# Attention's queries and keys turned on VectorE during the retention stage, and the opening stage reordered

## The chip, the cores and the metric

The kernel runs on one core of one Trainium2 chip. The metric is device time in microseconds: the median of a few runs of the whole program. The profile is of one further execution.

## The reference

One layer of a streaming encoder on 1024 tokens of width 1024, with 16 meta tokens in front. All mixers read the same normalised input through one projection, and their outputs go through one output projection. Cut to what matters here:

```python
u = rms_norm(h, ln_w[l])
(cx, cb, cc, cz, cq, ckv, krope, mz, rq, rk, rv, rz) = split(u @ w_in[l])
y_conv = short_conv_mixer(cx, cb, cc, cz, ...)
# attention: 8 heads of 96, v of 64, chunk-causal mask
q = rms_norm(rms_norm(cq) @ w_uq, q_norm);  k = rms_norm(concat(k_nope, k_r), k_norm)
s = einsum('bqhd,bkhd->bhqk', rope(q), rope(k)) * 96 ** -0.5
y_mla = einsum('bhqk,bkhd->bqhd', softmax(mask(s)), v) * silu(mz)
y_ret = retention_mixer(rq, rk, rv, rz, ...)       # 4 heads of 64, a state carried from chunk to chunk
h = h + concat(y_conv, y_mla, y_ret) @ w_out[l]
```

## The kernel before

All data are float32. A product of two float32 matrices is made of three matmuls (`mm3`, L109): each operand is split into a rounded part and a rest (`split`, L100: ScalarE makes the one, VectorE or GpSimd the other by subtraction), and high x high, high x low and low x high are summed in PSUM.

The program is written as one list of steps, and the framework lays out the order of each engine's queue when the program is built: an instruction that its plan holds ready may come ahead of others that stand earlier in the text, and the text decides between ready ones. Once laid out, each queue runs strictly in its order; SP's queue issues nearly all DMAs.

The stages, in the order of the profile:

- Opening, to 55 us (L170 to L260). TensorE warms up with `NW` matmuls on zeros (L175). Then 8 blocks of the input, each with its weights, are loaded and split, and the attention gates `mz` are summed over them: blocks 0 to 3 of 128 columns by two halves g of the tokens, each with a PSUM tile of its own. Blocks (0,0), (0,1), (1,0), (1,1), (2,0) run with the loads; (2,1) and block 3 come behind (`rest`, L179). Meanwhile x is read token by token for its sums of squares; `r` is the reciprocal norm of each token, and a matmul of ones with a diagonal matrix (L243) turns four tiles of it into a row over all partitions, `rb`. L253 to L260 make the gates of `mz` and store them. The weights of the next projection, `wA`, are loaded by `load_w` (L114): four (`NA`) early, four behind the gates (L270). They share 12 buffers with the weights of `mz`.
- Projection A, 55 to 121 us (L293 to L409): latents, queries, keys and values of attention, with norm and rotation. Queries and keys are stored to DRAM token by token, as `q_s` and `k_s` (L388, L368).
- Retention, 121 to 246 us (L423 to L532). For two pairs of heads u and nine tiles of tokens t, `r_proj` makes a projection of 24 matmuls; `step()` then runs what earlier tiles left for later: `r_rope` (rotation on VectorE, then two small transposes `rtp` on TensorE, L456), `r_score`, `r_out`. The weights of u = 1 are loaded during u = 0, those of the convolution during u = 1 (L528 to L532).
- Convolution, 246 to 345 us (L535 to L602), whose last part is interleaved with the start of attention (L797 to L815).
- Attention, 345 to 530 us, 8 heads of 8 tiles (L794 to L864). For each head `load_pair` (L542) has loaded queries and keys of two heads, token by token on the partitions. `qk_t` (L662) turns 512 tokens of one head with four TensorE transposes (L668) into PSUM, and splits them from there into `qT` or `kT`; the queries are scaled by `wqk`, the product of the two norm weights, in that split. It is called four times for each head (which of q and k, which half of the tokens), for heads 2 to 7 two heads ahead, after the tiles in `QK`. `score` makes the scores of one tile, `p_t` turns the softmax, `attend` multiplies with v. Part of the output projection (`partial`) fills in.
- Output projection, to the end.

The pool `hpp` (L71) has two buffers for each of the tags "q", "k" and "v". The tag "q" is used in turn by the input blocks, the attention weights `uq`, the queries of a pair, and late outputs.

## Time and profile before

| | us |
|---|---|
| median of 3 runs | 580.33 (579.04 to 581.69) |
| the profiled execution | 581.55 |
| its span, first to last instruction | 579.8 |
| TensorE busy | 569.8 |
| VectorE busy | 330.9 |
| ScalarE busy | 255.0 |
| GpSimd busy | 224.1 |

A busy time is the time in which at least one instruction of the engine is under way. Matmuls overlap one another, so the room that one takes in TensorE's queue is the distance from its start to the next start, not its duration. In the rows PE is TensorE, DVE VectorE, ACT ScalarE, POOL GpSimd, SP the queue of DMAs; L668 is line 668 of the program; `kTp<-ident,k` says that kTp is written and ident and k are read.

### The profile page before, as it was taken

Reading aid. Unit: us, or ns where it says so; the run is one execution under the profiler, and the core shown is the slowest. Engines: PE = TensorE matmul, PEld = TensorE weight load, DVE = VectorE, ACT = ScalarE, POOL = GpSimd, SP = SyncE. Lnnn points to the kernel's source line nnn. Section 1 sums busy time; section 2 is a strip of 40 time slices with the busy share of each in tenths; the row PEclk is TensorE's granted clock in tenths of the full one; section 3 lists DMA queues with packets and bytes.
Section 4 is the critical chain, followed back from the end, with each engine's and each line's share of the span. In section 5 each row is a group of like instructions: output and inputs, shape, how many; then the busy total and the mean of one; then the engine's idle time right before and its main releaser. Section 6 shows DMA issues by size and latency. Waiting matters only on the chain.

```text
span 579.8 us, 9595 instructions
## 1 busy us (share of the span) xinstructions
PE 569.8 (98%) x3401; PEld 481.7 (83%) x3401; DVE 330.9 (57%) x761; ACT 255.0 (44%) x616; POOL 224.1 (39%) x330
## 2 busy tenths in 40 slices
PE   8999999999999999999999999999999999999997
PEld 5877899988888888898898888898888888876886
DVE  5547768888536432553332667675757857664132
ACT  6765535665234332532010438475655646543000
POOL 2023258677103220151242968443524334624000
PEclk9999999999999999999999999999999999999999
DMA  8887513274703200130030648235112223113096
GB/s 326 289 265 241 182 67 120 108 224 158 234 1 92 74 0 19 54 110 18 20 97 1 199 145 273 73 103 171 56 38 73 77 71 128 37 68 116 1 301 224
DMA packets 46657, 70.39 MB, mean 121 GB/s; under 512 B 3792, under 2 KB 21840, under 8 KB 46480
## 3 DMA queue, kind: packets, MB, share of 16 engines
q1 hardware_dynamic: 43008, 63.47, 33.8%
q10 hardware_dynamic: 3600, 6.29, 2.9%
q8 instruction: 27, 0.44, 0.3%
q14 instruction: 22, 0.18, 0.1%
HBM read 48.75 MB, written 21.00 MB: 120 GB/s over the span
## 4 chain that ended last, share of the span: by engine, by line
PE 83%; DMA 9%; DVE 3%; ACT 2%; issue 2%; POOL 0%; SPq 0%; DVEq 0%; ACTq 0%; POOLq 0%
PE r L112 16%; PE S L112 9%; PE cv L112 8%; PE part L112 7%; PE A L112 6%; PE o L765 6%; PE pTp L724 5%; PE cz L112 4%; PE cb L112 4%; DMA out<-ot 4%; PE out L112 3%; PE qps L112 3%; DMA xs<-in_xT 2%; DMA xt<-in_x 2%; PE rsp L477 1%
## 5 line engine op out<-in xcount | busy, mean ns | idle before, releaser
L702 ACT ACTIVATE pr<-S,smx 128x144 f32<-128x144 f32 (+8 forms) x72 | 50.4, 701 | 27.3 <-DVE smx L693 13.4
L693 DVE TENSOR_REDUCE smx<-S 128x1 f32<-128x144 f32 (+8 forms) x72 | 49.8, 701 | 15.7 <-PE S L112 6.3
L710 POOL TENSOR_SCALAR pm<-pr,smx 128x16 f32<-128x16 f32 x64 | 18.4, 288 | 85.2 <-DVE smx L708 61.3
L711 POOL TENSOR_SCALAR pr<-pr,smx 128x128 f32<-128x128 f32 (+3 forms) x64 | 48.1, 752 | 0.6 <-DVE smx L708 0.6
L724 PE MATMUL pTp<-ident,pr 128*128 128x128 f32 x288 | 45.4, 274 | 1.5 <-ACT pt L730 1.4
L730 ACT COPY pt<-pTp 128x512 f32<-128x512 f32 (+2 forms) x64 | 31.8, 505 | 26.3 <-PE pTp L724 24.9
L451 POOL TENSOR_SCALAR kw<-qk,con 128x64 f32<-128x64 f32 (+1 forms) x36 | 13.8, 397 | 71.7 <-DVE qk L447 58.4
L724 PEld LDWEIGHTS pTp<-ident,pr 128*128 128x128 f32 x288 | 35.0, 140 | 7.0 <-POOL wol L104 1.8
L765 PEld LDWEIGHTS o<-pt,v 128*64 128x64 f32 x448 | 26.5, 137 | 12.1 <-issue 4.7
L765 PE MATMUL o<-pt,v 128*64 128x256 f32 (+2 forms) x448 | 36.2, 309 | 0.0
L112 PE MATMUL r<-wh_r,xal 128*128 128x512 f32 (+1 forms) x80 | 30.5, 381 | 0.0
L112 PE MATMUL r<-wh_r,xah 128*128 128x512 f32 (+1 forms) x80 | 30.4, 380 | 0.0
L112 PE MATMUL part<-woh,yh 128*128 128x512 f32 x64 | 30.1, 470 | 0.0
L112 PE MATMUL r<-wl_r,xah 128*128 128x512 f32 (+1 forms) x80 | 30.0, 375 | 0.0
L882 DVE SCALAR_TENSOR_TENSOR ot<-out,xr 128x512 f32<-128x512 f32 (+1 forms) x17 | 11.2, 660 | 31.1 <-DMA out<-ot 16.8
L112 PE MATMUL r<-wl_r,xbh 128*128 128x512 f32 x64 | 26.1, 409 | 0.0
L112 PE MATMUL r<-wh_r,xbh 128*128 128x512 f32 x64 | 25.7, 401 | 0.0
L112 PE MATMUL part<-wol,yh 128*128 128x512 f32 x64 | 25.5, 399 | 0.0
L112 PE MATMUL r<-wh_r,xbl 128*128 128x512 f32 x64 | 25.5, 398 | 0.0
L112 PE MATMUL part<-woh,yl 128*128 128x512 f32 x64 | 25.2, 394 | 0.0
L773 DVE TENSOR_TENSOR ym<-o,ym 64x256 f32<-64x256 f32 x32 | 13.5, 421 | 16.7 <-PE o L767 16.2
L104 POOL TENSOR_TENSOR wol<-wos,woh 128x512 fp32r<-128x512 f32 x16 | 20.4, 1291 | 2.6 <-ACT woh L103 2.6
(295 smaller groups left out, 1716.1 us busy)
## 6 DMA issues: line engine op xcount, KB each, us to landing
xt<-in_x SPq DMA_DIRECT2D x16, 256.0 KB, 4.5
ws_r<-in_win SPq DMA_DIRECT2D x16, 256.0 KB, 3.3
ws_c<-in_win SPq DMA_DIRECT2D x16, 256.0 KB, 2.9
wos<-in_wout SPq DMA_DIRECT2D x16, 256.0 KB, 3.8
xp<-in_x SPq DMA_DIRECT2D x16, 256.0 KB, 2.7
p_s<-xp SPq DMA_DIRECT2D x16, 256.0 KB, 2.0
xr<-p_s SPq DMA_DIRECT2D x15, 256.0 KB, 4.5
out<-ot ACTq DMA_DIRECT2D x15, 256.0 KB, 4.5
```

The source lines that it names most:

```text
L104: (lo_eng or nc.vector).tensor_tensor(lo, src, hi.bitcast(F32), op=ALU.subtract)
L112: nc.tensor.matmul(out, lhsT=x_, rhs=y_, start=first and i == 0, stop=last and i == 2)
L451: nc.gpsimd.tensor_scalar(kw[R, j], qk[R, 2 + j], con[R, kd0 + j:kd0 + j + 1], 1.0, op0=ALU.mult, op1=ALU.mult)
L693: nc.vector.tensor_reduce(sm[:, i // 2:i // 2 + 1], sp[:, :n, :w], axis=AX.XY, op=ALU.max, negate=True)
L702: e = nc.scalar.activation(pr[:, c0:c1].rearrange("p (b c) -> p b c", b=n), sp, AF.Exp, bias=mx, accum_out=sm[:, 5 + i:6 + i])
L710: nc.gpsimd.tensor_scalar(pm[(2 * h + t // 4) % 2][:, t % 4, :NM], pr[:, nk - NM:nk], sm[:, 9:10], 1.0, op0=ALU.mult, op1=ALU.mult)
L711: nc.gpsimd.tensor_scalar(pr[:, :nk - NM], pr[:, :nk - NM], sm[:, 9:10], 1.0, op0=ALU.mult, op1=ALU.mult)
L724: tr_ = nc.tensor.transpose(out=tp[:, b * P:b * P + P], in_=pr[:, c0:c0 + P], identity=ident)
L730: nc.scalar.copy(pt[:, b0:b0 + nb, tt], src)
L765: nc.tensor.matmul(op[64 * cg:64 * cg + 64, c0:c1], lhsT=lv, rhs=src[:, i_, c_], start=b == 0, stop=False)
L773: nc.vector.tensor_tensor(ys, op[64 * cg:64 * cg + 64, :256].rearrange("p (a c q) -> p a c q", a=2, q=64), ys, op=ALU.mult)
L882: nc.vector.scalar_tensor_tensor(ot, acc[:, c0:c1], 0.5, xt, op0=ALU.mult, op1=ALU.add)
```

## The change

- Weight vectors: the norm weights of queries and keys take two columns each of `vec`, so `wqk` has two columns, one for each of the first two groups of 32 features of a head.
- Opening: 11 warming matmuls instead of 8. Six of the eight weight blocks of (2,1) are placed after the first half of the row sums' input, the two matmuls with ones (`r_row`) follow, then the other two; block 3 runs weight by weight over both halves instead of half by half. The last four `wA` are loaded one by one ahead of each gate's block.
- Retention: after each of the 16 tile steps with t from 0 to 7, one or two parts of a `turn`. For each head pair, keys first: part 0 loads 1024 tokens x 192 columns from `k_s` or `q_s`; part 1 transposes all 32x32 blocks on VectorE; part 2, for queries, multiplies the first two groups of 32 features of each head by the weights on ScalarE (two instructions), and stores four times 32 partitions to a new DRAM tensor `T_s`, feature by feature. The third part of the last turn stands behind the first three quarters of the convolution.
- Attention: `load_head` loads 96 rows x 1024 tokens of each head's queries and keys from `T_s`, two heads ahead; `load_pair` loads values alone. `qk_t` splits straight from there, with the order of the tokens put right by the access pattern; its TensorE transposes and the scale are gone.

```diff
-    NA, NW, GA = 4, 8, 0
+    NA, NW, GA = 4, 11, 0
...
+    T_s = [dp.tile([4, 192, SEQ], F32, name=f"{c}T_s") for c in "qk"]
...
-    wqk = cp.tile([P, 1], F32, name="wqk")
+    wqk = cp.tile([P, 2], F32, name="wqk")
...
-        def rest(b, g, a):
-            for k in range(KT):
+        def rest(b, g, a, ks=range(KT)):
+            for k in ks:
...
+            if g == GA:
+                rest(2, 1, accs[2, 1], range(6))
             if g == 2:
                 break
+
+        def r_row(g):
 
             dg = work("t2", f"dg{g}").rearrange("p (t q) -> p t q", t=4)
...
-        rest(2, 1, accs[2, 1])
+        for g in range(2):
+            r_row(g)
+        rest(2, 1, accs[2, 1], range(6, KT))
         for g in range(2):
             accs[3, g] = ps0.tile([P, 512], F32, tag="rps", name=f"mz3{g}", bufs=2)
-            rest(3, g, accs[3, g])
+        for k in range(KT):
+            for g in range(2):
+                rest(3, g, accs[3, g], (k,))
         for b in range(4):
+
+            with tc.issue_after(last_t.ins):
+                wA.append(load_w("A", len(wA)))
...
     with tc.issue_after(last_t.ins):
-        wA += [load_w("A", k) for k in range(len(wA), KT)]
         nc.sync.dma_start(con, ins["con"])
...
+    turned = []
+
+    def turn(i, part):
+
+        hp, which = i // 2, 1 - i % 2
+        if part == 0:
+            src = hp_pool.tile([P, NT, 192], F32, tag="q", name=f"ts{i}")
+            nc.sync.dma_start(src, (q_s, k_s)[which].rearrange("t p c -> p t c")[:, :, hp * 192:hp * 192 + 192])
+            turned.append(src)
+        elif part == 1:
+            dst = hp_pool.tile([P, 6, NT * 32], F32, tag="q", name=f"td{i}")
+            nc.vector.transpose(dst.rearrange("p c (t k) -> p t c k", k=32),
+                                turned.pop().rearrange("p t (c k) -> p t c k", k=32))
+            turned.append(dst)
+        else:
+            dst = turned.pop()
+            if which == 0:
+
+                for c in range(2):
+                    nc.scalar.activation(dst[:, c::3], dst[:, c::3], AF.Copy, scale=wqk[:, c:c + 1])
+            to = T_s[which][hp].rearrange("(c f) (i r) -> i f c r", f=32, i=4)
+            for j in range(4):
+                nc.sync.dma_start(to[j], dst[32 * j:32 * j + 32])
+
     for u in range(2):
         for t in [8] + list(range(NT)):
             r_proj(u, t)
             step()
+            if t != 8:
+                i, part = divmod(u * NT + t, 2)
+                if part == 0 and i:
+                    turn(i - 1, 2)
+                turn(i, part)
...
+    raw = {}
+
+    def load_head(h):
+        for which in (1, 0):
+            x = hp_pool.tile([P, 1536], F32, tag="qk"[which], name=f"{'qk'[which]}{h}")[:96, :SEQ]
+            nc.sync.dma_start(x, T_s[which][h // 2, 96 * (h % 2):96 * (h % 2) + 96])
+            raw[h, which] = x.rearrange("p (i t k) -> p t i k", i=4, k=32)
+
     def load_pair(hp):
-        qt = hp_pool.tile([P, NT, 192], F32, tag="q", name=f"q{hp}")
-        kt = hp_pool.tile([P, NT, 192], F32, tag="k", name=f"k{hp}")
         vt = hp_pool.tile([P, NT, 128], F32, tag="v", name=f"v{hp}")
-        nc.sync.dma_start(kt, k_s.rearrange("t p c -> p t c")[:, :, hp * 192:hp * 192 + 192])
-        nc.sync.dma_start(qt, q_s.rearrange("t p c -> p t c")[:, :, hp * 192:hp * 192 + 192])
...
+    turn(NT - 1, 2)
+    for h in range(2):
+        load_head(h)
     pairs = [load_pair(0)]
...
         def qk_t(h, g, which):
-            qt, kt, _ = pairs[h // 2]
-            cs = slice(96 * (h % 2), 96 * (h % 2) + 96)
-            tp = pst("tq", f"{'qk'[which]}Tp{h}_{g}")
-            src = (qt, kt)[which]
-            for j in range(4):
-                nc.tensor.transpose(out=tp[:96, j * P:j * P + P], in_=src[:, 4 * g + j, cs], identity=ident)
-            if which == 0:
-                gs = slice(g * 512, g * 512 + 512)
-                split(qT[h % 2][0][:96, gs], qT[h % 2][1][:96, gs], tp[:96], scale=wqk[:96])
-            else:
-                gs = slice(NM + g * 512, NM + g * 512 + 512)
-                if g == 0:
-                    for i, m_ in enumerate((kmh, kml)):
-                        nc.gpsimd.tensor_copy(kT[h % 2][i][:96, :NM], m_[:, h].bitcast(F32))
-                split(kT[h % 2][0][:96, gs], kT[h % 2][1][:96, gs], tp[:96])
+            src = raw[h, which][:, 4 * g:4 * g + 4]
+            o = g * 512 + NM * which
+            dst = [x[:96, o:o + 512].rearrange("p (t i k) -> p t i k", i=4, k=32) for x in (qT, kT)[which][h % 2]]
+            if which == 1 and g == 0:
+                for i, m_ in enumerate((kmh, kml)):
+                    nc.gpsimd.tensor_copy(kT[h % 2][i][:96, :NM], m_[:, h].bitcast(F32))
+            split(*dst, src)
...
+            if t == 0 and h + 2 < H:
+                load_head(h + 2)
```

## Rows read from the trace of the kernel before

**Rows 1.** the page: busy us of each engine, share, instructions

```profile
PE 569.8 (98%) x3401; PEld 481.7 (83%) x3401; DVE 330.9 (57%) x761; ACT 255.0 (44%) x616; POOL 224.1 (39%) x330
```

**Rows 2.** the view of waits, TensorE: us in total, times, longest

```profile
PE A L112 <- ACT wh_A L103: 1.5, 1, 1.5
...
PE A L112 <- DVE wl_A L104: 0.4, 1, 0.4
PE rps L243 <- DVE vxe L248: 0.3, 1, 0.3
```

**Rows 3.** busy us by stretch: PE, PEld, DVE, ACT, POOL; clock, DMA, GB/s

```profile
150.00:180.00 30.00, 30.00 (x153) 25.01 (x152) 11.00 (x35) 10.12 (x30) 5.37 (x10) 1.00 0.20 65
...
210.00:246.00 36.00, 35.88 (x182) 29.75 (x181) 14.06 (x42) 13.15 (x37) 4.40 (x10) 1.00 0.09 30
360.00:520.00 160.00, 159.99 (x1263) 135.62 (x1261) 108.50 (x266) 92.54 (x226) 70.14 (x132) 1.00 0.25 79
```

**Rows 4.** groups of instructions on TensorE: busy us, mean ns, idle before

```profile
L668 PE MATMUL qTp<-ident,q 128*96 128x128 f32 x64 | 9.6, 273 | 0.0
L668 PE MATMUL kTp<-ident,k 128*96 128x128 f32 x64 | 9.6, 272 | 0.0
```

**Rows 5.** TensorE in order of time, attention: start us, us

```profile
378.51 0.60 PE L668 MATMUL kTp<-ident,k 128*96 128x128 f32 x4
378.94 0.71 PE L724 MATMUL pTp<-ident,pr 128*128 128x128 f32 x5
...
382.27 0.60 PE L668 MATMUL qTp<-ident,q 128*96 128x128 f32 x4
382.62 0.43 PE L112 MATMUL S<-kt0h,qt0h 104*128 104x400 f32 x1
382.89 0.35 PE L112 MATMUL S<-kt0l,qt0h 104*128 104x400 f32 x1
383.07 0.35 PE L112 MATMUL S<-kt0h,qt0l 104*128 104x400 f32 x1
```

**Rows 6.** tiles kt0l and qt0h: ns min/median/max, starts, shapes

```profile
L104 DVE TENSOR_TENSOR kt0l<-kTp,kt0h x8: 676/682/687, 325.4 to 458.8; 96x512 fp32r<-96x512 f32 x8
...
L106 ACT ACTIVATE qt0h<-qTp,wqk x8: 672/684/692, 325.3 to 461.1; 96x512 fp32r<-96x512 f32 x8
```

**Rows 7.** DMA issues by line: KB each, median us to landing

```profile
k_s<-kqo SPq DMA_DIRECT2D x8, 384.0 KB, 2.3
...
k<-k_s SPq DMA_DIRECT2D x4, 768.0 KB, 5.5
```

**Rows 8.** VectorE and TensorE in order of time, one retention tile

```profile
152.03 0.41 DVE L447 TENSOR_TENSOR qk<-qk 128x256 f32<-128x256 f32 x1
...
155.60 0.38 PE L456 MATMUL rtp<-ident,qk 128*128 128x128 f32 x2
```

**Rows 9.** TensorE in order of time, opening

```profile
5.96 1.65 PE L112 MATMUL mz<-xah,wh_mz 128*128 128x512 f32 x3 [1.18 <-ACT wh_mz L103]
...
9.97 1.16 PE L112 MATMUL mz<-xah,wl_mz 128*128 128x512 f32 x3
10.97 0.39 PE L112 MATMUL mz<-xbl,wh_mz 128*128 128x512 f32 x1
11.20 0.40 PE L112 MATMUL mz<-xbh,wl_mz 128*128 128x512 f32 x1
```

**Rows 10.** busy time by stretch, as rows 3, in the opening

```profile
6.00:8.00 2.00, 2.00 (x5) 1.61 (x6) 2.00 (x4) 1.07 (x2) 0.00 (x0) 1.00 1.04 418
```

**Rows 11.** VectorE in order of time, the first copy of projection A

```profile
62.88 0.30 DVE L307 COPY c<-A 16x160 f32<-16x160 f32 x1
```

**Rows 12.** busy time by stretch, as rows 3, around the gates

```profile
38.00:63.00 25.00, 22.76 (x115) 18.39 (x114) 19.31 (x35) 13.12 (x26) 6.66 (x7) 1.00 0.79 253
```

**Rows 13.** VectorE and GpSimd in order of time, late convolution

```profile
332.45 3.08 DVE L579 SCALAR_TENSOR_TENSOR yv<-ccs,vec,yv 128x512 f32<-128x512 f32 x1
...
332.43 2.55 POOL L104 TENSOR_TENSOR wol<-wos,woh 128x512 fp32r<-128x512 f32 x2
```

More of the change, by code (lines that the diff above doesn't have):

```diff
@@ L33 @@
 WTOT = _o
-V_LN, V_QA, V_KVA, V_QN, V_KN, V_CW, V_CB, V_RN = 0, 8, 10, 11, 12, 13, 19, 21
-NV = 22
+V_LN, V_QA, V_KVA, V_QN, V_KN, V_CW, V_CB, V_RN = 0, 8, 10, 11, 13, 15, 21, 23
+NV = 24
 C_TA = 0
@@ L286, in trunk @@
         nc.gpsimd.tensor_tensor(tabs[:, i], tab, wrow[:, None, i * 32:i * 32 + 32].to_broadcast([P, 9, 32]), op=ALU.mult)
-    nc.gpsimd.tensor_tensor(wqk, vec[:, V_QN:V_QN + 1], vec[:, V_KN:V_KN + 1], op=ALU.mult)
+    nc.gpsimd.tensor_tensor(wqk, vec[:, V_QN:V_QN + 2], vec[:, V_KN:V_KN + 2], op=ALU.mult)
     def small(tag, name, n):
@@ L540, in feat @@
         return pp
+    raw = {}
[4 more added lines that the diff above has]
+            raw[h, which] = x.rearrange("p (i t k) -> p t i k", i=4, k=32)
     def load_pair(hp):
-        qt = hp_pool.tile([P, NT, 192], F32, tag="q", name=f"q{hp}")
-        kt = hp_pool.tile([P, NT, 192], F32, tag="k", name=f"k{hp}")
         vt = hp_pool.tile([P, NT, 128], F32, tag="v", name=f"v{hp}")
-        nc.sync.dma_start(kt, k_s.rearrange("t p c -> p t c")[:, :, hp * 192:hp * 192 + 192])
-        nc.sync.dma_start(qt, q_s.rearrange("t p c -> p t c")[:, :, hp * 192:hp * 192 + 192])
         nc.sync.dma_start(vt, v_s[:SEQ, hp * 128:hp * 128 + 128].rearrange("(b p) c -> p b c", p=P))
-        return qt, kt, vt
+        return vt
     ccs = {}
@@ L746, in attend @@
             nj = 4 * g + 4
-            pt, vt = pts.pop((h, g)), pairs[hp][2]
+            pt, vt = pts.pop((h, g)), pairs[hp]
             op = pst("o", f"o{h}_{g}")
@@ L964, in _layout @@
     qn, kn = A["q_norm"][0], A["k_norm"][0]
-    vec[:, V_QN:V_KN + 1] = 1.0
-    vec[:64, V_QN], vec[:64, V_KN] = qn[:64], kn[:64]
+    for o, n in ((V_QN, qn), (V_KN, kn)):
+        vec[:, o:o + 2] = np.tile(n[:64].reshape(2, 32).T, (4, 1))
     for u in range(2):
```

## The prediction

> **What bounds the kernel now.** I read the page first: TensorE is busy for 569.8 of 579.8 us, VectorE for 57%, ScalarE for 44%, GpSimd for 39% [rows 1]. A busy TensorE is not yet a full one, so the waits come next: all that it waited for under its own name is a few stalls, 1.9 us at the first A projection and 0.3 us at the row sums among them [rows 2]. By stretch it is full in the retention stage and in attention, while VectorE is busy 11.0 of 30 us and 14.1 of 36 us in the one, and 108.5 of 160 us in the other [rows 3]. So an instruction taken off TensorE's queue shortens the kernel by the room it took there, and work put on VectorE in the retention stage has room, if nothing waits behind it.
>
> The profiled execution took 581.55 us, 1.75 us of it outside its 579.8 us span; the median of the runs is 580.33. I make the sum on the profiled one and take 1.2 us off at the end.
>
> **Part 1: the transposes leave TensorE.** `qk_t` loses its four transposes, 32 calls in all, 128 instructions, each shown at 272 to 273 ns, 19.2 us busy together [rows 4]. That is the time they are in flight, not the room they take: matmuls overlap. The room is read from start to start. The group of four keys starts at 378.51 and what follows it at 378.94: 0.43 us. The queries start at 382.27 and the next score matmul at 382.62, 0.35 us, but that matmul then holds the queue 0.27 us where the next one, of the same shape, takes 0.18 (382.62, 382.89, 383.07): a switch from this kind of matmul to that kind costs 0.09 us, together 0.44 [rows 5]. 32 groups x 0.43 us = 13.8 us. Bounds: 32 x 0.35 = 11.2 us, and 19.2 us if the busy time were the room. I take 13.8; the rows are next to each other, so they decide. Of these, 8 groups (heads 0 and 1) lie in the convolution, 3.4 us, and 24 in attention, 10.3 us.
>
> What is late next in attention: VectorE would have 108.5 us of work in 149.7 us, 72% instead of 68% [rows 3]. The splits stay, with their source in SBUF instead of PSUM; for queries the scale is gone, so a scaled copy becomes a copy. I cost them at nothing, covered by those 41 us; without the cover see the second rival.
>
> **Part 2: the turning in the retention stage.** Eight turns (four head pairs, keys and queries). Each is one load of 768 KB, one VectorE transpose of 128x1536, for queries two ScalarE scalings of 128x512, and four stores of 192 KB from 32 partitions each, all DMAs on SP's queue. The trace of before has no such transpose. The nearest row is a VectorE subtraction of 512 elements, 0.68 us [rows 6]: three times that is 2.0 us; bounds 1.0 (half) and 4.1 us (double). Eight cost 16 us on VectorE (8 to 33), whose free time in 150:180 alone is 19 us and in 210:246 another 22 [rows 3]. A scaling costs about the 0.68 us of the present scaled copy [rows 6], eight of them 5.5 us of ScalarE, which is busy a third of that stage [rows 3]. The load is the one that `load_pair` makes now, 5.5 us to landing. A store has the 384 KB one of 2.3 us beside it [rows 7]; four are between 2.3 us (all at once) and 9.2 (one after another). One turn is then 5.5 + 2.0 + 2.3 = 9.8 to 5.5 + 4.1 + 1.4 + 9.2 = 20.2 us. The next load waits only for the transpose ahead of it (two buffers), so eight take 8 x 7.5 = 60 us at best, and 162 us at worst. From 150 they end between 210 and 312 us. The first pair is wanted late in the convolution, the other pairs in attention, after 360. DMA is 20% busy in 150:180 and 9% in 210:246 [rows 3]: the load at 5.5 us and the stores disturb little there.
>
> The stores are weighed against a page. The Trainium skill, "SBUF — State Buffer", section "Door 1: The DMA port swizzle", says that 32 partitions reach half of the ports that 128 reach, and its closing rules ask for one transfer over 128 partitions in place of several. Its rule speaks against four stores of 32; a store would by it take about twice its time, an estimate; no row of before stores from 32 partitions. The 9.2 us bound has room for that, so the sum is the same by either.
>
> What the added waits hold up: the transpose waits on VectorE for its load, and behind it stand the four rotary operations on the next tile, for which TensorE's two small transposes (`rtp`) wait. In the row the last of the four ends at 152.44 and `rtp` starts at 155.60 [rows 8]: 3.1 us of slack a tile, over the 2.0 us of the transpose. On SP the stores stand ahead of the weight loads of units r1 and c0. r1 is needed at once when the second half of the stage begins; I allow 0.8 us lost there (bounds 0 and 5.5, one load).
>
> **Part 3: the opening.** Three more warming matmuls fill the idle 1.18 us before the first `mz` matmul. The first twelve `mz` matmuls (four runs of three; the first and the last stand there) take from 5.96 to 10.97, 0.42 us each, and the next 0.23 [rows 9]: TensorE at 1.2 GHz and then at 2.4, though the granted clock of the stretch reads 1.00 [rows 10]. At 0.23 the twelve would take 2.8 us, so 2.2 us are at stake. The clock rose after TensorE had worked without a gap from 5.96 on; with the gap filled it works without one from the start. Bounds 0 and 2.2; I take 1.5, since the rise may still come a little after 5.96. The Trainium skill, "TensorE: Matmul & The Clock Gate", part 1, says that the point of the rise differs from run to run, and that one kernel showed 6, 11 or 14 slow matmuls; by it the gain could be anything in those bounds, an estimate, and this one execution can't tell.
>
> The reordering puts 18 matmuls of block (2,1) ahead of the two row sums, so these no longer stop the queue: 0.3 us. The last four A weights are fetched and split between the gates instead of behind them, and block 3 runs weight by weight, which frees the buffers that those splits need: the 1.5 + 0.4 us stall goes [rows 2]. Together 1.5 + 0.3 + 1.9 = 3.7 us. But VectorE copies the first A result only at 62.88 [rows 11], and in 38:63 it is busy 19.3 of 25 us [rows 12]; TensorE, earlier by 3.7 us, meets this copy. I take 3.0 (bounds 0 and 4.4).
>
> **Sum:** 13.8 + 3.0 - 0.8 = 16.0 us. 581.55 - 16.0 = 565.5 for an execution like the profiled one, 564.3 for the median.
>
> **Rivals.**
> 1. The opening gives nothing: the clock rises where it did, and VectorE's copy holds A where it was. For it: the 19.3 of 25 us. Against: most of VectorE's idle time there is the very wait for the late A weight. 564.3 + 3.0 = 567.3 us.
> 2. VectorE binds in attention. The split's subtraction now reads two SBUF operands. One such operation of before, beside GpSimd work with two SBUF inputs, took 3.08 us [rows 13]; the present subtraction, one operand in PSUM, takes 0.68 [rows 6], 2.4 less. 24 of them (four for each of heads 2 to 7), all hit, are 58 us: 166 us of VectorE in a stage of 150, and it would decide from 41 us on, 1.7 each. GpSimd is busy 44% of the stage [rows 3], so I price it at 1.0 each, 25 us, which doesn't fill VectorE but delays softmax rows; half of the 10.3 us lost: 569.5 us. The Trainium skill, "SBUF — State Buffer", section "Who interferes with whom", states this as a rule (two SBUF inputs on VectorE contend with a GpSimd instruction that reads SBUF); the 3.08 us row agrees.
> 3. Slower than before: VectorE's queue stands at each turn. If a transpose reaches the head of the queue when its load has only been issued, it holds the rotary operations for 5.5 + 2.0 = 7.5 us, 4.4 beyond the slack, eight times: 35 us, 599 us. It turns slower than before from a hold of 5.1 us (3.1 + 16/8). For it: the load is queued on SP among other things, and one step earlier is all the distance that the code gives it. Against: a step of this stage is 24 matmuls of 0.23 us [rows 9], 5.5 us, and small ones besides, so at least the landing.
> 4. Better: the opening gives its 4.4 and nothing is lost at r1, which is 562.1; and with `qTp` and `kTp` gone the PSUM bank that they share with attention's output is free, so that 24 groups give nearer the 0.60 us for which they show busy [rows 5] than 0.43, some 3 us more: 559 us.
>
> **How the numbers follow.** Chances: the forecast 0.62, the first rival 0.13, the second 0.10, the third 0.07, the fourth 0.08. The forecast's own bounds are 564.3 - 3 (opening at its top, nothing lost at r1) and + 5 (r1 or the small end of part 1). The range is 557 to 573: it takes in rivals 1, 2 and 4 and leaves out the third and some tail. About 0.5% is what a measurement of this kernel can tell from no change. Faster by more: all but the third rival and a bad second, 0.90; within: 0.03; slower: 0.07.
>
> **What would show it.** Right: no `qTp` or `kTp` under TensorE; attention shorter by some 10 us and the convolution by 3; TensorE without new idle time in 150:246; transposes near 2 us each; `mz` at 0.23 us from near 6 us on; no wait of A for its weights. Wrong: TensorE waiting for `rtp`, or for r1 weights, in the retention stage; subtractions of 1.5 us and more in attention beside longer softmax waits; stores of the turned tiles landing after 300 us.

## The result, and the profile after

The changed kernel takes 594.41 and 596.69 us in two executions (two more, 864.45 and 685.35, ran at a lower granted clock and are left out), against 579.68 us for the kernel before beside it: 1.0269 times the time (1.0209 to 1.0329). It is slower, where 564.3 us and faster were forecast. Run again on another occasion it takes 596.07 us against 580.07 (1.0277, 1.0246 to 1.0308); the profile read below is of that run, with a span of 593.8 us.

Where the time went is read from the start of the first matmul of each stage, in us, and of the last instruction:

| | projection A | retention | convolution | output | end | retention lasts | convolution and attention last |
|---|---|---|---|---|---|---|---|
| before | 54.9 | 121.4 | 245.6 | 531.4 | 579.8 | 124.2 | 285.8 |
| after | 52.9 | 120.6 | 261.8 | 545.7 | 593.8 | 141.2 | 283.9 |

The opening and A give 0.8, convolution and attention 1.9, the output stage 0.3, and the retention costs 17.0: 14.0 us slower in sum. The view by stretch of the kernel after (columns as [rows 3]) shows the place:

```profile
150.00:180.00 30.00, 28.59 (x142) 23.17 (x141) 14.98 (x36) 9.68 (x29) 2.42 (x8) 1.00 0.58 157
180.00:210.00 30.00, 25.79 (x122) 20.17 (x121) 16.35 (x28) 10.84 (x25) 8.62 (x10) 0.89 0.68 193
210.00:246.00 36.00, 32.02 (x147) 25.22 (x145) 14.32 (x38) 9.78 (x28) 5.33 (x10) 0.95 0.55 153
...
374.00:534.00 160.00, 158.71 (x1162) 128.63 (x1163) 113.55 (x268) 95.14 (x231) 74.33 (x136) 1.00 0.28 89
```

TensorE, full there before, is idle 9.6 us between 150 and 246, and the granted clock reads 0.89 and 0.95 in the two later stretches. Over the whole stage (120.6 to 261.8) it is idle 9.7 us instead of 0.1, and busy 131.5 us instead of 124.1 with nearly the same matmuls, at a mean granted clock of 0.96 instead of 1.00: together the 17.0 us. VectorE is far from full. What it waits for itself (waits of VectorE, 118 to 264; us in total, times, longest) is the answer:

```profile
DVE td L547 <- DMA ts<-q_s: 11.0, 2, 5.7
DVE td L547 <- DMA qT_s<-td: 8.3, 3, 5.3
...
DVE td L547 <- issue: 5.8, 1, 5.8
...
DVE td L547 <- DMA ws_c<-in_win: 4.4, 1, 4.4
```

and the page's row of the transpose (busy us, mean ns, idle before):

```profile
L547 DVE STREAM_TRANSPOSE td<-ts 128x1536 f32<-128x1536 f32 x8 | 14.2, 1779 | 31.2 <-DMA ts<-q_s 11.0
```

`td<-ts` is the transpose: VectorE stood 31.2 us in front of the eight: for the load, for the stores that hold the buffer, once for nothing that the profile names (`issue`), and once by the profile for a weight load. In these last two the turn's own load landed 0.2 and 0.03 us before the transpose began, so they are read as waits for the load as well: five waits and 22.9 us for loads, three and 8.3 us for stores. One turn in order of time, on SP, VectorE, ScalarE and TensorE:

```profile
155.37 2.34 SPq L558 DMA_DIRECT2D kT_s<-td  x4
157.82 0.81 SPq L543 DMA_DIRECT2D ts<-q_s  x1
...
158.59 0.42 DVE L459 TENSOR_TENSOR qk<-qk 128x256 f32<-128x256 f32 x1
164.26 1.78 DVE L547 STREAM_TRANSPOSE td<-ts 128x1536 f32<-128x1536 f32 x1 [5.25 <-DMA ts<-q_s]
165.96 0.53 DVE L501 SCALAR_TENSOR_TENSOR state<-state,con,rup 64x64 f32<-64x64 f32 x2
...
166.08 1.33 ACT L555 ACTIVATE td<-td,wqk 128x512 f32<-128x512 f32 x2 [5.65 <-DVE td L547]
...
166.64 0.46 PE L497 MATMUL rup<-rt,kw 128*128 128x128 f32 x2 [0.70 <-DVE state L501]
```

The load is issued at 157.82, behind the four stores of the turn before, and VectorE reaches the transpose at 159.0. It stands until 164.26, and so does ScalarE in front of the scaling. The state update (`state`, behind the transpose on VectorE's queue) comes only at 165.96, and TensorE has to wait for it. The two largest of TensorE's own waits in the stage (118 to 264):

```profile
PE rop L506 <- DVE qs L490: 5.6, 4, 2.3
PE yp L530 <- POOL rwk L525: 2.1, 2, 1.8
```

### The profile page after: what moved, and what is told of

Its sections match the earlier page's. It is cut to its first block, busy times and chain, and to the rows that moved or that the text cites. A ratio compares the mean times of both kernels' runs of the same rounds, so it can differ in the third digit from the quotient of the medians.

```text
span 862.6 us, 9413 instructions
## 1 busy us (share of the span) xinstructions
PE 857.1 (99%) x3276; PEld 574.0 (67%) x3276; DVE 347.7 (40%) x769; ACT 265.4 (31%) x624; POOL 225.6 (26%) x330
## 4 chain that ended last, share of the span: by engine, by line
PE 99%; ACT 0%; DVE 0%; issue 0%; DVEq 0%
PE r L114 18%; PE S L114 9%; PE cv L114 9%; PE mz L114 9%; PE part L114 7%; PE A L114 7%; PE out L114 7%; PE o L805 6%; PE pTp L764 6%; PE cb L114 4%; PE cz L114 4%; PE qps L114 3%; PE rsp L489 1%; PE kps L114 1%; PE vps L114 1%; PE rop L506 1%
## 5 line engine op out<-in xcount | busy, mean ns | idle before, releaser
L764 PE MATMUL pTp<-ident,pr 128*128 128x128 f32 x288 | 60.5, 344 | 0.0
L805 PE MATMUL o<-pt,v 128*64 128x256 f32 (+2 forms) x448 | 51.5, 389 | 0.0
L805 PEld LDWEIGHTS o<-pt,v 128*64 128x64 f32 x448 | 30.6, 154 | 20.7 <-issue 8.7
L114 PE MATMUL r<-wh_r,xah 128*128 128x512 f32 (+1 forms) x80 | 44.1, 554 | 0.0
L114 PE MATMUL r<-wl_r,xah 128*128 128x512 f32 (+1 forms) x80 | 43.7, 546 | 0.0
L114 PE MATMUL r<-wh_r,xal 128*128 128x512 f32 (+1 forms) x80 | 43.1, 539 | 0.0
L114 PE MATMUL r<-wh_r,xbh 128*128 128x512 f32 x64 | 38.3, 599 | 0.0
L114 PE MATMUL r<-wl_r,xbh 128*128 128x512 f32 x64 | 38.1, 596 | 0.0
L114 PE MATMUL r<-wh_r,xbl 128*128 128x512 f32 x64 | 37.2, 582 | 0.0
L114 PE MATMUL qps<-uq,ct 128*128 128x384 f32 x96 | 30.0, 480 | 0.0
L501 DVE SCALAR_TENSOR_TENSOR state<-state,con,rup 64x64 f32<-64x64 f32 x32 | 8.9, 280 | 50.0 <-PE rop L492 31.2
```

The lines of the kernel that those rows point to most:

```text
L114: nc.tensor.matmul(out, lhsT=x_, rhs=y_, start=first and i == 0, stop=last and i == 2)
L501: nc.vector.scalar_tensor_tensor(stt[js, js], stt[js, js], con[js, C_G + u:C_G + u + 1], up[js, js], op0=ALU.mult, op1=ALU.add)
L764: tr_ = nc.tensor.transpose(out=tp[:, b * P:b * P + P], in_=pr[:, c0:c0 + P], identity=ident)
L805: nc.tensor.matmul(op[64 * cg:64 * cg + 64, c0:c1], lhsT=lv, rhs=src[:, i_, c_], start=b == 0, stop=False)
```

## The experiments

Each time stands beside the kernel before on the same chip (580 to 581.5 us).

**Is it the warming, the opening, or the turning?** e1 is the changed kernel once more, e2 has its warming undone:

> The changed kernel again. Its profile showed a granted clock of 1.00 to 4 us, 0.60 in 4 to 6 us and 0.56 from then on. Theory W (the three more warming matmuls, which leave TensorE no gap at its start, make the granted clock fall): below 1.00 again from some 4 to 6 us on, a time from 590 us up. Rival D (a TensorE with 128 transposes fewer is fuller, and the clock falls for that): also below 1.00, but the fall should then come in attention, not at 4 us. Rival C (a disturbance of that one chip, nothing of the kernel): 1.00 and some 564 us.

```diff
-    NA, NW, GA = 4, 11, 0
+    NA, NW, GA = 4, 8, 0
```

> The changed kernel with 8 warming matmuls instead of 11, all else kept. Theory W: the gap is back, granted clock 1.00 throughout, 562 to 569 us (the prediction without its 1.5 us for the clock). Rival D, and a rival O (the reordered opening is the cause): the clock is below 1.00 as before, 590 us or more.

e3 is the kernel before with 11 warming matmuls, e4 the changed kernel with the opening of before:

> The kernel before with 11 warming matmuls instead of 8, all else kept. Theory W: the granted clock falls below 1.00 at 4 to 6 us here too, and the time goes to 600 us or more, with a wide spread. Rivals D and O: clock 1.00, 578 to 580 us (the first mz matmuls reach 0.23 us up to 2.2 us sooner).

> Only the turning of queries and keys and what follows from it (new tensors, loads by head, splits without TensorE), with the opening of the kernel before and 8 warming matmuls. Theory W: clock 1.00, and 580 - 13.8 + 0.8 = 567 us, bounds 565 to 573. Rival D: clock below 1.00, 590 us or more. Rival O: as theory W.

596.07, 594.73, 583.15 and 592.9 us; ratios 1.0277, 1.0255 (1.0234 to 1.0276), 1.0056 (1.0036 to 1.0075) and 1.0226 (1.0202 to 1.0249). The turning by itself costs 12.8 us, and its retention lasts 138.0 us. My first suspicion, a clock that the warming makes fall, didn't survive e2 and e3: with 8 warming matmuls the changed kernel is as slow, and the kernel before with 11 is 3.1 us slower, not 20 or more. These 3.1 us are clear of noise, though, and rivals D and O had expected none: the warming that was to gain 1.5 us gained nothing. Rival D's time came in e2 and e4, its reason didn't: the granted clock over 374 to 534 reads 1.00.

**The attention's half, the transposes, the transfers, and the lead.** All runs from here on have the opening of before and 8 warming matmuls, unless the text says otherwise, so that those with a turning stand against e4 (592.9 us). e6 leaves out the turning and reads row-major data:

```diff
-                if part == 0 and i:
-                    turn(i - 1, 2)
-                turn(i, part)
...
-            nc.sync.dma_start(x, T_s[which][h // 2, 96 * (h % 2):96 * (h % 2) + 96])
+            row = (q_s, k_s)[which].rearrange("t p c -> (t p c)").rearrange("(f s) -> f s", s=SEQ)
+            nc.sync.dma_start(x, row[96 * h:96 * h + 96])
```

> Leaves out the turning itself (no loads, transposes, scaling or stores in the retention stage); the attention reads each head's 96 rows of 1024 from the row-major queries and keys as if they were transposed and unscaled, so its output is not the reference's. Opening as before, 8 warm-up matmuls. It prices the attention's half of the change by itself. Theory Q (the attention runs out of covering work and gives back most of the TensorE time that it gains, whatever the retention does): retention 124 to 125 us as in the kernel before, first convolution matmul to first output matmul 283 to 285 us against 285.8 before, total 577 to 580 us. Rival R (the attention lost its gain only because the retention sent late stores and loads ahead of it): the full 10 to 12 us of TensorE time comes out, total 568 to 570 us.

579.14 us (0.9989, 0.9974 to 1.0005); retention 124.3, convolution and attention 284.0. Theory Q holds: with a quiet retention the attention gives 1.8 us in these two profiles, not 12, and the whole kernel 0.9 us, which is within noise.

e7 drops the transpose alone:

```diff
-            nc.vector.transpose(dst.rearrange("p c (t k) -> p t c k", k=32),
-                                turned.pop().rearrange("p t (c k) -> p t c k", k=32))
+            pass
```

> The turning without its VectorE step: the eight loads, the scaling and the 32 stores stay, the loaded tile itself is scaled and stored, so the output is not the reference's. Theory L (VectorE's in-order queue stands at each transpose until its load has landed, and TensorE's chain behind it stands too): without the transpose nothing on VectorE waits for a load, the retention falls from 138 to 125 to 128 us, total 579 to 583 us. Rival T (the 12.6 MB of extra transfers, or the issue on SP's queue, delay the stage whatever VectorE does): retention stays at 135 to 139, total 590 to 594 us. Rival H (the 1.8 us hold of VectorE costs the time, load or no load): as theory L here.

593.71 us, retention 137.1. This run didn't decide: the scaling now waits for the load itself, and ScalarE's queue stands in VectorE's place (waits of ScalarE, 118 to 262):

```profile
ACT ts L542 <- DMA ts<-q_s: 24.0, 4, 8.8
```

e8 keeps only the transposes, of a tile that never changes:

```diff
+                    nc.gpsimd.memset(still, 0.0)
...
+                    nc.vector.transpose(dst.rearrange("p c (t k) -> p t c k", k=32),
+                                        still.rearrange("p t (c k) -> p t c k", k=32))
```

> The turning without its transfers: the eight VectorE transposes stay where they are, always of one tile that lies in SBUF from the start; loads, scaling and stores are left out and the attention reads row-major data as if transposed, so the output is not the reference's. Theory L: the hold of 1.8 us lies within the 3.1 us of slack, retention 125 to 128 us, total 578 to 581 us. Rival H: the hold alone makes the stage 135 to 139 us, total 588 to 592 us. Rival T: as theory L here.

580.32 us (1.0002, 0.9982 to 1.0021), retention 124.2. The tile's row and the stretch in which most of the transposes lie:

```profile
L561 DVE STREAM_TRANSPOSE td<-ts x8: 1764/1767/1771, 141.4 to 163.3; 128x1536 f32<-128x1536 f32 x8
```

```profile
150.00:180.00 30.00, 30.00 (x154) 25.08 (x154) 21.34 (x46) 9.87 (x29) 5.03 (x13) 1.00 0.18 54
```

TensorE loses nothing, though VectorE is held 14 us in 24. With nothing to wait for, the framework drew the eight together, so this prices the hold, not its place in each step.

e9 issues the load a step earlier:

```diff
+                    turn(i, 1)
+                    if i + 1 < NT:
+                        turn(i + 1, 0)
```

> The turning whole, but each load is issued right behind the transpose of the turn before, one step earlier and ahead of that turn's stores on SP's queue. Theory L: the load has landed when VectorE comes to the transpose, retention 126 to 129 us, total 580 to 584 us. Rivals T and H: retention stays at 135 to 139, total 590 to 594 us.

587.97 us (1.0124, 1.0079 to 1.0169), retention 134.1: about a third of the loss came back, less than theory L had forecast and more than its rivals. The load no longer ends the longest waits; the stores that hold the second buffer do (waits of VectorE, 118 to 262):

```profile
DVE td L537 <- DMA kT_s<-td: 13.9, 3, 4.9
DVE td L537 <- DMA qT_s<-td: 8.4, 3, 4.2
```

**One head at a time, with lead and buffers; and the transfers without any wait.** e10 turns a head's 768 columns a step:

```diff
+        i = s - 2
+        if 0 <= i < 2 * H:
+            td[i] = hp_pool.tile([P, 1024], F32, tag="v", name=f"td{i}")[:, :768].rearrange("p (c r) -> p c r", c=3)
...
+        i = s - 3
+        if 0 <= i < 2 * H:
+            x, h = td.pop(i), i // 2
```

> The turning whole, in 16 pieces of one head's 768 columns instead of eight of 1536, one piece a step, with two buffers for the loaded and two for the turned data, so that a load is issued two steps before its transpose and a store a step before its buffer is wanted again. Same bytes moved. Theory L (an in-order engine queue stands for a landing): no engine waits for a landing any more, retention 125 to 128 us, total 578 to 583 us. Rival T (the traffic itself, or the issue of it on SP's queue, costs the time): retention 132 to 139, total 587 to 594 us.

579.21 us (0.9978, 0.9955 to 1.0002), retention 124.3: the whole loss is gone, with the same bytes moved. VectorE still stands in front of transposes, 8.9 us in all (waits of VectorE, 118 to 262), but never longer than 2.2 at once, and TensorE waits for nothing in the stage. Stretches, and the transposes:

```profile
150.00:180.00 30.00, 30.00 (x152) 24.98 (x151) 18.88 (x47) 13.54 (x38) 4.07 (x9) 1.00 0.86 233
180.00:210.00 30.00, 30.00 (x161) 24.68 (x161) 21.21 (x47) 14.49 (x36) 9.73 (x14) 1.00 0.89 254
```

```profile
L533 DVE STREAM_TRANSPOSE td<-ts x16: 967/978/979, 152.7 to 210.6; 128x768 f32<-128x768 f32 x16
```

DMA is busier here (0.86 and 0.89) than in the changed kernel (0.58 and 0.68), and TensorE doesn't notice: traffic alone isn't the price. In step s it loads piece s, transposes piece s - 2 and stores piece s - 3. The smaller pieces, the lead and the buffers came together in this run; which of them would do alone was not tried.

e12 is e7 without the scaling:

```diff
-                for c in range(2):
-                    nc.scalar.activation(dst[:, c::3], dst[:, c::3], AF.Copy, scale=wqk[:, c:c + 1])
```

> The turning's transfers alone: the eight loads and 32 stores stay, transposes and scaling are left out and the loaded tile is stored as it is, so the output is not the reference's and no compute engine waits for a landing. Theory L: retention 125 to 128 us, total 579 to 583 us. Rival T (traffic or issue on SP's queue costs the time by itself): retention 132 to 139, total 587 to 594 us.

591.01 us (1.0185, 1.0141 to 1.0229), retention 135.9: a miss for theory L, and what rival T had forecast. With no engine to hold them back the turns follow each other as fast as their buffers allow, and the last of the eight weights of the stage's second half stands behind them on SP: it is issued at 189.8 (182.1 in e10) and lands 6.8 us later. Wait of TensorE, and stretch:

```profile
PE r L114 <- ACT wh_r L105: 8.3, 1, 8.3
```

```profile
180.00:210.00 30.00, 21.37 (x108) 17.00 (x107) 11.13 (x30) 9.08 (x24) 5.14 (x8) 0.83 0.99 269
```

So the same transfers can cost 11 us in a second way, by bunching. The changed kernel's TensorE doesn't wait for these weights by name, though its last one is issued at 191.3. Theory L stands for it, by its waits, e8, e9 and e10. The hold by itself is out (e8), and the same traffic need not cost anything (e10); but e12 shows that the transfers can cost as much without any wait on VectorE, so a share of the late weight is not excluded.

**The opening alone.** e5, with 8 warming matmuls and no turning:

```diff
+            if g == GA:
+                rest(2, 1, accs[2, 1], range(6))
...
+                wA.append(load_w("A", len(wA)))
```

> The opening's reordering alone: mix-gate matmuls between the row sums, each of A's loads issued inside its stage, 8 warm-up matmuls, no turning. The prediction's term: 3.0 us gained, total 577.0 us. Rival 1 (the opening gives nothing, which the spread of the opening between profiles of the same code suggests): 579 to 581 us. Rival N (the new order costs time, as the changed kernel with 8 warm-ups against the turning alone, 594.7 against 592.9, suggests): 581 to 583 us.

580.44 us (0.9994, 0.9965 to 1.0023): nothing, as in the first rival of the prediction. TensorE's wait for the A weights here, and ScalarE's row that ends it; then the same two of the kernel after:

```profile
PE A L112 <- ACT wh_A L103: 1.7, 1, 1.7
```

```profile
57.38 0.54 ACT L103 CAST wh_A<-ws_A 128x416 fp32r<-128x416 f32 x1 [2.83 <-DMA ws_A<-in_win]
```

```profile
PE A L114 <- ACT wh_A L105: 3.4, 1, 3.4
```

```profile
57.36 0.54 ACT L105 CAST wh_A<-ws_A 128x416 fp32r<-128x416 f32 x1 [2.96 <-DMA ws_A<-in_win]
```

The split of the last A weight starts at 57.4 in both, and at 57.5 before (its load issued at 53.7, 53.0 and 53.6): the reordering didn't move that load. What TensorE gains ahead of it, it waits longer there.

**Why the attention gives so little: order, entry, or chain?** In the laid-out queue the value matmuls (`o`) stand in 37 runs instead of 19, so the framework's order was the first suspect, and the wait at the entry the second. e11 was meant for the entry:

```diff
-    while cuts:
-        cuts.pop(0)()
-    y_split(0)
     conv_cb(1, 1)
```

> The attention alone (as the run that leaves out the turning and reads row-major data as if transposed, 579.1 us), with the GpSimd splits of the first output weights and of y moved behind the splits of head 1's queries and keys. Theory X (VectorE's subtraction of two operands in SBUF takes 3.6 us instead of 0.68 while GpSimd runs its own, which makes the convolution's gate matmul wait 2.6 us and TensorE's clock fall behind it): the long subtraction falls to about 0.7 us, the wait goes, total 575 to 577 us. Rival (the subtraction is late for another reason, or the wait moves on to the next use): total 578 to 580 us.

580.7 us (1.0, 0.9978 to 1.0021), and the long subtraction still 3.60 us: the framework put the GpSimd work where it had been, so this edit tried nothing.

e13 (e6 with it) and e14 (e10 with it) hold TensorE's old order; `chain` lists its matmuls as the kernel before has them:

```diff
+    for a, b in zip(chain, chain[1:]):
+        tc.add_manual_dep(b, a.name, mybir.DependencyInfo(mybir.DependencyClass.NoSync, mybir.DependencyReason.DATA), reason="order")
```

> The attention alone again (turning left out, row-major data read as if transposed, 579.1 us), with TensorE's queue from the first score to the last attention matmul held in the order that it has in the kernel before, the transposes of queries and keys taken out of it; the other queues are laid out by the framework around it. Theory P (the framework laid TensorE's queue out anew when the transposes went, with the value matmuls in 37 runs instead of 19, and the new order eats the gain): first score to first output matmul falls from 200.1 to 189 to 193 us, total 569 to 573 us. Rival C (the softmax chain of VectorE, ScalarE and GpSimd sets the pace whatever the order): 197 to 201 us, total 577 to 580 us. In between, each has a share.

> The whole turning in one-head pieces (579.2 us), computing the full result, with TensorE's queue in the attention held in the order of the kernel before without the transposes. Theory P: total 569 to 573 us, faster than the kernel before by 7 to 11 us. Rival C: 577 to 580 us.

584.39 and 583.27 us (1.0056, 1.0032 to 1.0081; 1.0027, 1.0002 to 1.0052): the old order is no better; of the first only the time is used. In the second, heads 2 to 5 last 22.7 us each, from the first softmax transpose of one to that of the next, against 23.6 before and 23.4 in e10. The four groups of a head fill 1.5 us there, so the old order lets 0.9 of it come out, and the framework's order 0.2: in these heads the order is about half of what is missing. But the entry, from the first score to head 1's first softmax transpose, takes 46.1 us instead of 35.4, with pauses of TensorE of 3.0, 2.4 and 2.1 us and a granted clock of 0.66 over 347.7 to 357.7. Theory P's times fail; as the run holds the entry as well, its total doesn't price the order by itself.

e15 mends the entry of e10; e16 adds the old order from head 2 on:

```diff
+    with tc.issue_after(ccs["last"].ins):
+        for g in range(2):
+            qk_t(1, g, 1)
```

> The whole turning in one-head pieces (579.2 us), with one order set by hand on VectorE: head 1's low halves stand behind the convolution's last coefficient, for which the gate matmul waits at the attention's entry (2.6 us of wait and 1.7 us of slowed matmuls in every run with the new attention). Theory E (the entry's share of the give-back is VectorE's order): the wait goes, first score to first output matmul falls from 200.1 to 195 to 198 us, total 575 to 577.5 us. Rival C (the softmax chain takes it back in head 0): 199 to 201 us, total 578 to 580 us.

> The same, and TensorE's queue from head 2 on held in the order of the kernel before without the transposes; there each of the four middle heads took 22.6 us against 23.5 before and 23.4 in the new order (mean of 22.3, 23.9, 23.7 and 23.7). Theory P in its smaller form (the new order costs some 0.8 us a head, the rest of the give-back is the softmax chain): 3 us less than the run beside it, total 572 to 574.5 us. Rival C: no less than the run beside it.

585.89 and 586.69 us (1.0082, 1.0051 to 1.0113; 1.0085, 1.0055 to 1.0115). The wait at the gate matmul went, and in e15 the first softmax transpose comes 14.4 us behind the first score instead of 18.3 in e10, but head 0 then takes 29.8 us instead of 21.5: TensorE now waits there for GpSimd's scaling (2.3 us), ScalarE's exp (1.6) and VectorE's `yv` (1.4). Mending one wait made later ones longer.

e17 is e14, and e18 the kernel before, with exp freed from the maximum:

```diff
-                e = nc.scalar.activation(pr[:, c0:c1].rearrange("p (b c) -> p b c", b=n), sp, AF.Exp, bias=mx, accum_out=sm[:, 5 + i:6 + i])
+                e = nc.scalar.activation(pr[:, c0:c1].rearrange("p (b c) -> p b c", b=n), sp, AF.Exp, bias=half_neg[:, :1], scale=1.0 / 16, accum_out=sm[:, 5 + i:6 + i])
```

> The turning in one-head pieces with TensorE's old order (583.3 us), with the softmax chain shortened by one link: the row maximum is still taken on VectorE, but ScalarE's exp reads a constant instead and doesn't wait for it, and takes a sixteenth of the score, so the output is not the reference's. TensorE's order is the same as in the run that it stands against. Theory C (the chain score, maximum, exp, sum, scaling on three engines now ends last, and takes back what the transposes left): first score to first output matmul falls from 204.9 us by 5 to 10 us, total 573 to 578 us. Rival (what binds is the width of an engine or TensorE itself, and the wait only moves): falls by under 2 us, total 581 to 583.5 us.

> The kernel before with the same link taken out of the softmax chain, and TensorE's order in the attention held as it was; its exp takes a sixteenth of the score without the maximum, so the output is not the reference's. Theory C: here the transposes of queries and keys fill TensorE while the chain runs, so the link costs little: falls by 0 to 2 us, total 578 to 581 us. If it falls as far as the other run does, the chain was the bound before the change as well, and the transposes never stood on the path.

586.5 and 582.11 us (1.0084, 1.0053 to 1.0114; 0.9998, 0.9971 to 1.0024): neither gains (first score to first output matmul: 207.1 instead of 204.9, and 201.1 instead of 200.2), so the wait of exp for the maximum by itself is not the link that counts. The maximum reads the score's PSUM too, and may hold the buffer as before; a run that moves the maximum itself was not made.

What the traces do show is where the room goes. TensorE's order is the same in these two stretches, of the kernel before and of the turning in the old order (e14), apart from the transposes:

```profile
427.17 0.60 PE L668 MATMUL kTp<-ident,k 128*96 128x128 f32 x4
427.61 0.27 PE L724 MATMUL pTp<-ident,pr 128*128 128x128 f32 x1
427.89 0.45 PE L112 MATMUL S<-kt0h,qt0h 104*128 104x400 f32 x1
```

```profile
432.52 0.27 PE L780 MATMUL pTp<-ident,pr 128*128 128x128 f32 x1
433.16 0.45 PE L141 MATMUL S<-kt0h,qt0h 104*128 104x400 f32 x1 [0.37 <-ACT pr L757]
...
440.97 0.27 PE L793 MATMUL mTp<-ident,pm 128*128 128x128 f32 x1
441.48 0.47 PE L141 MATMUL S<-kt0h,qt0h 104*128 104x456 f32 x1 [0.24 <-ACT pr L757]
```

Before, 0.72 us from `kTp` to the score, of which 0.28 from `pTp`; after, 0.64 from `pTp` to it. Of the group's 0.44 us 0.36 became a wait of the score for ScalarE's exp of an earlier one. At the second place `mTp` to the score takes 0.51 us; before, this room held `mTp` and a group of `qTp`, also some 0.50. In this head two of the four groups come out, two turn into waits.

Over the whole attention the waits of TensorE's weight loads show it best (PEld, from the first score to the output). Before, and the one-head turning (e10) in the framework's own order, the largest rows of each:

```profile
PEld o L765 <- issue: 4.7, 15, 0.4
PEld pTp L724 <- POOL wol L104: 1.8, 1, 1.8
...
PEld S L112 <- ACT pr L702: 1.2, 6, 0.2
```

```profile
PEld o L791 <- issue: 5.0, 23, 0.4
PEld pTp L750 <- issue: 3.0, 11, 0.7
PEld cz L114 <- DVE ccs L593: 2.8, 1, 2.8
PEld S L114 <- ACT pr L728: 2.3, 7, 0.8
PEld pTp L750 <- DVE pt L754: 1.3, 3, 0.5
```

All rows of the view sum to 11.7 us before and to 20.7 in e10: 9.0 us more, 2.8 of it in one wait and the rest in many small ones, of which 3.5 are `issue`, where the profile names no engine. The one large wait, for `ccs`, is made on VectorE at the entry (here in e6; VectorE, then GpSimd):

```profile
323.22 3.60 DVE L106 TENSOR_TENSOR kt0l<-k,kt0h 96x512 fp32r<-96x512 f32 x1
...
323.62 2.55 POOL L106 TENSOR_TENSOR wol<-wos,woh 128x512 fp32r<-128x512 f32 x2
```

Behind it the clock falls: the 24 gate matmuls take 7.2 us from start to start instead of 5.6, eight of them 0.43 us each (1.2 GHz) instead of 0.23 (2.4); the granted clock reads 0.90 over 328 to 345 in e10.

The whole account can be made from each matmul's start to the next one's, between the first score and the first output matmul (200.2 us before, 200.1 in e10). The groups of queries and keys filled 11.0 us of it before (12.5 with the four groups ahead of the first score) and nothing after. In their place the softmax transposes fill 33.0 us instead of 28.6, the value matmuls 41.5 instead of 38.7, the scores 59.7 instead of 57.1, the gate `cz` 7.2 instead of 5.6, `mTp` 0.4 more and `part` 1.1 less. The value matmuls' 2.8 us belong to the order: e14, in the old one, has 38.7 again. And the entry alone, to head 1's first softmax transpose, takes 39.9 us instead of 35.4, though eight groups (3.3 us) left it and only value matmuls of 3.8 us came into it.

## Why the prediction was wrong, step by step

- **What bounds the kernel** ("an instruction taken off TensorE's queue shortens the kernel by the room it took there"): this sentence failed in attention. TensorE was full there in part because the transposes filled moments in which its next work wasn't ready, and part of their room went to the framework's new order. A busy share can't show this: with 12.5 us of work gone TensorE still reads 158.71 of 160 us.
- **Part 1**, 13.8 us: the size of the room was nearly right (12.5 us measured over all groups, without the switch), but 0.2 to 2.5 us arrived: convolution and attention last 283.3 to 284.0 us with the new attention in the framework's order, and 285.8, 284.2 and 284.9 with the old one (before, e3, e5). I took the small rows beside a group as proof that its room would come out whole; they say only that nothing waited while it was there. "VectorE would have 108.5 us in 149.7" asked for capacity; no engine is full, and the waits come from the order in which single results arrive.
- **Part 2**: transpose 1.78 us (forecast 2.0), scaling 0.72 (0.68), loads 5.7 in the middle (5.5), four stores 5.3 to 6.5 from the first issue to the last landing in the five turns that show it (2.3 to 9.2), the last transpose at 228 us (the end forecast at 210 to 312): all sizes held. The step that failed is "3.1 us of slack a tile, over the 2.0 us of the transpose". It set the instruction's duration against the slack and left out its waiting for the load, priced at nothing. The third rival had the mechanism, at 0.07. Its "Against" counted one step as lead; the load lost that lead on SP, issued behind the four stores of the turn before it. Its price, 35 us, was too high: the stage lost 13.8 to 17.0. And it named only the load; in e9 the stores that hold the second buffer keep VectorE waiting up to 4.9 us at a time. For the r1 weights, 0.8 us forecast, TensorE has no wait by name in the changed kernel, and one of 8.3 us in e12.
- **Part 3**, 3.0 us: nothing of it came (e5 580.44 us without the extra warming, e3 583.15 with it alone). The clock's part was a chance of the one execution read. Of 16 profiles with 8 warming matmuls six have 6 to 10 slow `mz` matmuls at the start and ten at most one; e1 and e3, with 11, have at most one. The slow matmuls vary, as "TensorE: Matmul & The Clock Gate" of the Trainium skill, part 1, says. The forecast "the 1.5 + 0.4 us stall goes" failed: the last weight's load didn't move. Nor did the row sums always stop holding the queue (0.3 us): e1 waits 0.6 us there and e2 3.1.
- **The second rival**, VectorE's subtractions: right in kind. All 32 took 31.3 us in e10 against 22.8 before, 0.27 us more each; priced at 1.0. The 3.60 us row beside GpSimd's split agrees with the rule that the Trainium skill, "SBUF — State Buffer", section "Who interferes with whom", states. The one wait of TensorE that is traced to such a row lies at the entry; e15 took that wait away and gained nothing.
- **The stores from 32 partitions**: the rule of "Door 1: The DMA port swizzle" on the same page of the Trainium skill was weighed at no change of the sum. No run here prices it; with 64 such stores in e10 the stage lasts as long as before.
- **The signs**: transposes near 2 us showed, no `qTp` or `kTp` showed, and TensorE waiting in the retention stage was named as the sign of wrong. It waited most before `rop` (5.6 us) and `yp` (2.1), and hardly before `rtp` (0.7).

What stays open is which link of the softmax work sets the attention's pace now. Order, entry and the maximum's wait were tried, and none gives the time back; no run had the old order behind a quick entry. No version tried beats the kernel before by more than the noise.

## What to carry to other kernels

Price a new instruction on an in-order queue by what it waits for, counted from when its load is really issued and its buffer really free, not by its duration; with pieces of half the size, two steps of lead and two buffers on either side the same turning costs nothing here. Work taken off a full engine is worth its room only where what follows is ready: leave the work out in one run first, as e6 does, and see whether the time comes out. A stall ends with one event; if the change doesn't move that event, earlier work only makes the stall longer.

## What the runs showed of the hardware

- VectorE's transpose of 32x32 blocks, fp32, takes 1.78 us for 128x1536 and 0.98 for 128x768. By these two sizes alone that is 0.18 us and 1.04 ns a column.
- The same subtraction of 512 columns from SBUF takes 0.68 us at its shortest and up to 3.60 beside GpSimd's.
- A pause of 2.6 us on TensorE in the attention's entry (e10) was followed by eight matmuls at 1.2 GHz; the kernel before, without that pause, has none there.
- Stores of 96 KB from 32 partitions (e10) land after 3.7 and 3.9 us in the middle (keys, queries), those of 192 KB (the kernel after) after 3.3 and 4.1: in these stages the time doesn't follow the size.
